# RWKV triangular systems in a hybrid decoder step: DRAM transfers replaced by VectorE 32x32 block transposes, and key norms from four products with a tile of ones

## Chip, cores and metric

The kernel runs on one core of one Trainium2 chip. The metric is the device time of one execution in microseconds (us). TensorE is called PE, VectorE DVE, ScalarE ACT, GpSimd POOL and SyncE SP, as in the profile. SP issues nearly all DMA transfers.

## The reference

One inference step of a two-layer trunk with width 1024, for one prompt of 16 + 1024 tokens and 8 sample sequences of 8 tokens: 1104 columns in all. Layer 0 is a gated DeltaNet, layer 1 is RWKV-7 time mixing. The change is in layer 1. Cut to what matters there:

```python
xs = xn[None] + xx[None] * mu[:, None, None, :]          # six mixes with the token before
rkvz = jnp.einsum('sbtd,sde->sbte', xs[:4], w_rkvz)      # r, k, v, z
...
kk = l2norm((k * k_k).reshape(B, T, H, N))               # H = 16 heads of N = 64
k = k * (1.0 + (a - 1.0) * k_a)
decay = jnp.exp(-jnp.exp(w))
b_h = kk * a_h
def step(S, inp):
    r_t, k_t, v_t, d_t, kk_t, b_t = inp
    S = (S * d_t[:, :, None, :]
         + jnp.einsum('bhvk,bhk->bhv', S, -kk_t)[..., None] * b_t[:, :, None, :]
         + v_t[..., None] * k_t[:, :, None, :])
    return S, jnp.einsum('bhvk,bhk->bhv', S, r_t)
```

The kernel does not step token by token. It takes chunks of 64 tokens. Within a chunk, the term with `-kk_t` makes a triangular system of 64 x 64 for each head. The kernel inverts those systems ahead of the recurrence.

## The kernel before

Tokens lie along the free axis, features along the partitions, and a tile holds a pair of heads: head 0 in partitions 0 to 63, head 1 in 64 to 127. The columns are cut into three segments (`SEGS`: 384, 384 and 336). One segment of one head pair is an **item**: 3 x 8 = 24 items, each with 6 chunks of 64 tokens.

The order of instructions on each engine is fixed when the program is built. A planner simulates the engines and takes ready instructions by their place in the program. Each engine then works strictly in its own order, and waits where a semaphore is not yet there. Only the recurrence has PE's order written by hand.

Layer 1 (`layer1`, L1801) runs in three parts:

1. `keys_decay_rate` (L1165) projects the keys and makes decay and rate; it stores them to DRAM as `kd`, `csd` and `ad`.
2. The loop at L1811 runs 24 projections of 128 features each (`project`, L1152): r, then v, then z. Every weight tile of 128 x 512 is loaded (`wraw`), split by ACT into `whi` and by POOL into `wlo`, and multiplied in three products for precision. Before each kind, `mix` (L1017) makes the mixed inputs on ACT, DVE and POOL. Between the projections, after numbers 1, 4, 7, 10 and 13, one batch of the inverses is put into the program (`rwkv_inverse`, L1293): five items, four in the last.
3. `wave` (L1841) runs the recurrence, with the output projection filled in. For each item `rwkv_front` (L1340) loads what the earlier parts left.

`rwkv_inverse` does this for each item of a batch:

- It loads `cs`, `a` and `k` (three DMAs of 192 KB, the next item's ahead of time). ACT scales `k` by `k_k` (tile `skk`) and makes two exponentials (`sDp`, `siD`) and the squares (`sgl`).
- DVE makes `sal` = `skk` x `sDp` (L1285); POOL corrects the first columns (L1286, L1288) and multiplies `skk` by `a` (L1310); DVE multiplies that by `siD` (L1311). Both results are stored to DRAM (`ald`, `bkd`).
- PE makes the 64 x 64 products of both (12 matmuls, PSUM tile `fL`), and the sums of squares with the mask `hmask` (one matmul of 384 columns, PSUM tile `frss`).
- ACT copies the products (L1322), POOL masks the first chunk of segment 0 (L1324), and they go to the DRAM tensor `rltd`. DVE copies the norms (L1327), and they go to `rssd`.

Then, for the batch:

- `block_scale` (L489) loads the norms back in two layouts; one is transposed by PE (`fbpp`).
- `inverse_blocks` (L457) loads the two diagonal 32 x 32 blocks of each system with one system to a partition (`invA`, at most 120 partitions) and the off-diagonal block `L21`. DVE scales `invA` (L470). `inverse32` (L442) inverts all blocks at once in 31 steps of two DVE instructions each, between `invA` and `invT`.
- ACT copies the inverse with its two free axes exchanged (L472). It is stored to DRAM (`r_u`), and so is the plain one (`r_t`). Both are loaded back into `T1n` (two DMAs a batch, L480) and `sTT` (four DMAs an item, L486), whose zero quarter POOL clears (L484).
- `inverse_merge` (L506) makes the off-diagonal block of the inverse with 2 x 12 small matmuls an item (PSUM tiles `mY`, `mU`), a DVE scaling (L518) and two ACT copies. POOL scales the result by the norms (L1336), and one DMA stores it to `ttd` (L1337).

Of the kernel before, what the change touches and what calls it, by code (L numbers as in the profile page):

```python
# [35 lines left out]
class Builder:  # L36
# [76 lines left out]
    def consts(self):  # L113
# [15 lines left out]
        self.hmask = t(cp, [128, 2], "hmask")  # L129
        nc.gpsimd.memset(self.hmask, 0.0)  # L130
        for h in (0, 1):
            nc.gpsimd.memset(self.hmask[64 * h:64 * h + 64, h:h + 1], 1.0)
# [323 lines left out]

    def inverse_blocks(self, name, ltd, scale_blk, pool, TT, T1n, L21, nth):  # L457

        nc = self.nc
        nb = 4 * nth
        for p in (0, 1):
            nc.sync.dma_start(L21[64 * p:64 * p + 32], ltd[:, 64 * p:64 * p + 32, 32:64].rearrange("c s i -> s c i"))
        A = self.t(pool, [128, 1024], "invA", 2)[0:nb]
        Av = A.rearrange("p (s i) -> p s i", i=32)
        fl = ltd.rearrange("t q i -> (t q) i").rearrange("(c s) i -> c s i", s=64)
        for r in (0, 1):
            nc.sync.dma_start(Av[2 * nth * r:2 * nth * (r + 1)], fl[:, 32 * r:32 * r + 32, 32 * r:32 * r + 32])
        nc.vector.tensor_tensor(Av, Av, scale_blk.unsqueeze(1).broadcast_to([nb, 32, 32]), op=ALU.mult)  # L470
        Tv = self.inverse32(Av, nb, pool)
        nc.scalar.copy(Av, Tv.rearrange("p i j -> p j i"))  # L472
        ud = self.dram([nb, 1024], name + "_u")
        t1d = self.dram([nb // 2, 1024], name + "_t")
        nc.sync.dma_start(ud, A)
        nc.sync.dma_start(t1d, Tv[0:nb // 2].rearrange("p i j -> p (i j)"))
        uv = ud.rearrange("(r c p) (s i) -> r p s c i", r=2, p=2, s=32)
        tv = t1d.rearrange("(c p) (s i) -> p s c i", p=2, s=32)
        for p in (0, 1):
            nc.sync.dma_start(T1n[64 * p:64 * p + 32], tv[p])  # L480
        for n, tt in enumerate(TT):
            k = tt.shape[1]
            for p in (0, 1):
                nc.gpsimd.memset(tt[64 * p + 32:64 * p + 64, :, 0:32], 0.0)  # L484
                for r in (0, 1):
                    nc.sync.dma_start(tt[64 * p + 32 * r:64 * p + 32 * r + 32, :, 32 * r:32 * r + 32],  # L486
                                      uv[r, p][:, k * n:k * n + k])

    def block_scale(self, ssd, col, pool):  # L489


        nc = self.nc
        n = col.shape[1]
        row = self.t(pool, [128, 128], "invR", 1)[0:n]
        nc.sync.dma_start(row, ssd)
        ps = self.ps("f", 2, "bpp")
        self.transpose(ps[0:128, 0:n], row)
        blk = self.t(pool, [4 * n, 32], "bblk", 2)
        for r in (0, 1):
            nc.sync.dma_start(blk[2 * n * r:2 * n * r + 2 * n], ssd.rearrange("c (p r i) -> r (c p) i", p=2, r=2)[r])  # L500
        for x, y in ((col, ps[0:128, 0:n]), (blk, blk)):
            nc.vector.tensor_scalar(x, y, 1e-6, None, op0=ALU.add)
            nc.vector.reciprocal(x, x)
        return blk

    def inverse_merge(self, L21, TT, T1n, scale_col, pool, th0, n):  # L506
# [15 lines left out]
        for c in range(n):  # L522
            for p in (0, 1):
                a = 64 * p
                self.mm(uv[a:a + 32, c, :], Y[a + 32:a + 64, c, :], TT[a + 32:a + 64, c, 32:64])
        for p in (0, 1):
            a = 64 * p
            self.act(TT[a:a + 32, :, 32:64], uv[a:a + 32], AF.Identity, scale=-1.0)

# [682 lines left out]
    def rwkv_masks(self, ap, first=False):  # L1212
# [14 lines left out]
        if first:  # L1227
            self.m_strs2 = t(ap, [128, 64], "m_strs2")
            mask(self.m_strs2, True)
            return  # L1230
# [17 lines left out]
    def rwkv_open(self):  # L1248
        self.rk2 = self.t(self.cp, [128, 144], "rk2")
        self.csd, self.ad, self.rd, self.vd, self.zd, self.kd = (self.dram([8, 128, 1152], n) for n in  # L1250
                                                                 ("csd", "ad", "rd", "vd", "zd", "kd"))
        self.ttd, self.ald, self.bkd = (self.dram([24, 128, 384], n) for n in ("ttd", "ald", "bkd"))

    def rwkv_load(self, n, pool, tag, names):
        nc, t = self.nc, self.t
        s, p = divmod(n, 8)
        c0 = SEGS[s][0]
        ld = {}
        for nm in names:
            d = {"cs": self.csd, "a": self.ad, "r": self.rd, "v": self.vd, "k": self.kd}[nm]  # L1260
            ld[nm] = t(pool, [128, 384], tag + "ld" + nm, 2 if nm in "rv" or tag == "s" else 1)
            nc.sync.dma_start(ld[nm], d[p][:, c0:c0 + 384])
        return ld

    def rwkv_keys(self, p, ld, pool, tag):

        nc, t = self.nc, self.t
        kk = t(pool, [128, 384], tag + "kk", 2)
        self.act(kk, ld["k"], AF.Identity, scale=self.pcol["rwkv_k_k"][:, p:p + 1])
        return kk, *self.rwkv_decays(ld, pool, tag)  # L1270

    def rwkv_decays(self, ld, pool, tag):

        nc, t = self.nc, self.t
        Dp, iD = t(pool, [128, 385], tag + "Dp", 1), t(pool, [128, 384], tag + "iD", 1)
        nc.gpsimd.memset(Dp[:, 0:1], 1.0)
        self.act(Dp[:, 1:385], ld["cs"], AF.Exp, scale=-self.DEC)
        self.act(iD, ld["cs"], AF.Exp, scale=self.DEC)
        return Dp, iD

    def alpha(self, al, kk, Dp, s, eng):

        nc = self.nc
        c6 = lambda x: x.rearrange("p (c k) -> p c k", k=64)
        eng.tensor_tensor(al, c6(kk), c6(Dp[:, 0:384]), op=ALU.mult)  # L1285
        nc.gpsimd.tensor_copy(al[:, :, 0:1], c6(kk)[:, :, 0:1])  # L1286
        if s == 0:
            nc.gpsimd.tensor_copy(al[:, 0, :].rearrange("p (b r) -> p b r", r=8)[:, :, 0:1],  # L1288
                                  kk[:, 0:64].rearrange("p (b r) -> p b r", r=8)[:, :, 0:1])
# [3 lines left out]
    def rwkv_inverse(self, b, pool):  # L1293

        items = range(5 * b, min(5 * b + 5, 24))
        nth = 6 * len(items)
        nc, t = self.nc, self.t
        ltd, ssd = self.dram([nth, 128, 64], f"rltd{b}"), self.dram([nth, 128], f"rssd{b}")
        for q, n in enumerate(items):
            s, p = divmod(n, 8)  # L1300
            names = ("cs", "a", "k")
            ld = self.ahead or self.rwkv_load(n, pool, "s", names)
            kk, Dp, iD = self.rwkv_keys(p, ld, pool, "s")

            self.ahead = self.rwkv_load(n + 1, pool, "s", names) if n < 23 else None
            sq = t(pool, [128, 384], "sgl", 2)
            self.act(sq, kk, AF.Square)
            al = t(pool, [128, 6, 64], "sal", 1)
            self.alpha(al, kk, Dp, s, nc.vector)
            nc.gpsimd.tensor_tensor(kk, kk, ld["a"], op=ALU.mult)  # L1310
            nc.vector.tensor_tensor(kk, kk, iD, op=ALU.mult)  # L1311
            nc.sync.dma_start(self.ald[n], al.rearrange("p c k -> p (c k)"))
            nc.sync.dma_start(self.bkd[n], kk)
            gp = self.ps("f", 2, "L")
            ssp = self.ps("f", 2, "rss")
            for c in range(6):
                for h in (0, 1):
                    a = 64 * h
                    self.mm(gp[a:a + 64, 64 * c:64 * c + 64], kk[a:a + 64, 64 * c:64 * c + 64], al[a:a + 64, c, :])
            self.mm(ssp[0:2, 0:384], self.hmask, sq)  # L1320
            gl = t(pool, [128, 6, 64], "sgl", 2)
            nc.scalar.copy(gl, gp[:, 0:384].rearrange("p (c i) -> p c i", i=64))  # L1322
            if s == 0:
                nc.gpsimd.tensor_tensor(gl[:, 0, :], gl[:, 0, :], self.m_strs2, op=ALU.mult)  # L1324
            nc.sync.dma_start(ltd[6 * q:6 * q + 6].rearrange("c q i -> q c i"), gl)
            kc = t(pool, [2, 384], "rkc", 1)
            nc.vector.tensor_copy(kc, ssp[0:2, 0:384])  # L1327
            nc.sync.dma_start(ssd[6 * q:6 * q + 6].rearrange("c (h i) -> h c i", h=2), kc.rearrange("h (c i) -> h c i", c=6))
        rk2 = self.rk2[:, 30 * b:30 * b + nth]
        blk = self.block_scale(ssd, rk2, pool)  # L1330
        TT = [t(pool, [128, 6, 64], "sTT", 3) for _ in items]
        T1n, L21 = t(pool, [128, 30, 32], "T1n", 1), t(pool, [128, 30, 32], "L21", 1)
        self.inverse_blocks(f"r{b}", ltd, blk, pool, TT, T1n[:, 0:nth], L21[:, 0:nth], nth)
        for q, n in enumerate(items):
            self.inverse_merge(L21, TT[q], T1n, rk2[:, 6 * q:6 * q + 6], pool, 6 * q, 6)
            nc.gpsimd.tensor_tensor(TT[q], TT[q], rk2[:, 6 * q:6 * q + 6].unsqueeze(2).broadcast_to([128, 6, 64]), op=ALU.mult)  # L1336
            nc.sync.dma_start(self.ttd[n], TT[q].rearrange("p c k -> p (c k)"))  # L1337


    def rwkv_front(self, p, s):  # L1340
# [11 lines left out]
        ld = self.rwkv_load(P.n, fp, "f", ("cs", "k", "a", "r", "v"))  # L1352
# [7 lines left out]
        nc.sync.dma_start(AR[:, 0].rearrange("p c k -> p (c k)"), self.ald[P.n])  # L1360
# [616 lines left out]
```

## Time and profile before

| | |
|---|---|
| Time, median of 3 runs | 2362.39 us (2358.83 to 2364.0) |
| Time of the profiled execution | 2362.64 us |
| Mean granted PE clock of the span | 0.964 |
| First and last DVE step of the RWKV inverses (start) | 1545.2 and 1820.8 us |
| First load of the recurrence (`fldk`) | 1854.8 us |
| DMA, whole span | 308.89 MB in 499719 packets, 208089 of them under 512 bytes |

The span is the time from the first to the last instruction. In the page, times of engines are busy times; "share" is busy time over the span. Rows by groups of instructions read: line, engine, operation, tile written and tiles read with their shapes, count, busy us, mean ns of one, and after the second bar the idle time of the engine just before them with what ended it. Rows by stretch give the length, then the busy time of each engine in the order of the heading, the granted PE clock, the share of the DMA engines and GB/s. Rows of waits give total us, times, and the longest. `PEld` is PE's weight load. PE records come in pairs here: a float32 matmul leaves two.

### The profile page before, as it was taken

What the parts mean: (1) busy time and instruction counts of PE and PEld (TensorE: products, weight loads), DVE (VectorE), ACT (ScalarE), POOL (GpSimd) and SP (SyncE); (2) the same over time, 40 slices, a digit from 0 to 9 for tenths busy, and PEclk for the clock granted to TensorE, in tenths of its full rate; (3) what the DMA queues carried; (4) which work ended last, traced back from release to release, by engine and by line L of the source; (5) the groups of instructions that cost most, each with busy time, mean ns of one, the idle gap of its engine ahead of it and who ended that gap; (6) DMA issues with size and microseconds to landing.
All of it is one profiled execution on the core that took longest, in us unless ns stands there. A gap on an engine that the chain in (4) does not pass through costs nothing. (4 is left out here: it accounts for less than half of the span.)

```text
span 2360.9 us, 54503 instructions
## 1 busy us (share of the span) xinstructions
PE 2167.1 (92%) x19737; PEld 1961.9 (83%) x19737; DVE 1571.2 (67%) x4219; ACT 1282.6 (54%) x3599; POOL 949.4 (40%) x1318
## 2 busy tenths in 40 slices
PE   6989999999999999999999999999888888899886
PEld 5888989889898989898989998887777866778775
DVE  6878677685858686774345833479878456667754
ACT  5455545564656555456333746646444355677763
POOL 3445333443435353434232523446445423344433
PEclk9999999999999999999999999998999998999998
DMA  3423332323233333335152145577774654677753
GB/s 113 107 76 104 88 94 78 101 75 105 78 101 91 90 102 88 109 90 184 48 163 83 52 163 175 182 199 197 188 181 130 178 160 143 178 220 227 215 153 126
DMA packets 499719, 308.89 MB, mean 131 GB/s; under 512 B 208089, under 2 KB 484826, under 8 KB 499450
## 3 DMA queue, kind: packets, MB, share of 16 engines
q1 hardware_dynamic: 499450, 305.41, 45.6%
q8 instruction: 156, 2.56, 0.5%
q14 instruction: 113, 0.93, 0.1%
HBM read 209.97 MB, written 95.33 MB: 129 GB/s over the span
## 5 line engine op out<-in xcount | busy, mean ns | idle before, releaser
L90 POOL TENSOR_TENSOR wlo<-wraw,whi 128x512 fp32r<-128x512 f32 (+2 forms) x252 | 332.4, 1322 | 359.8 <-ACT whi L86 334.4
L76 PE MATMUL d<-xc,whi 128*128 128x384 f32 (+2 forms) x910 | 260.2, 344 | 8.1 <-ACT whi L86 3.6
L86 ACT CAST whi<-wraw 128x512 fp32r<-128x512 f32 (+2 forms) x252 | 151.7, 603 | 138.8 <-PE dq L76 50.7
L419 DVE SCALAR_TENSOR_TENSOR cvy<-raw,cw,cvy 128x408 f32<-128x408 f32 (+2 forms) x288 | 178.3, 632 | 15.7 <-ACT cvy L62 13.8
L452 DVE TENSOR_TENSOR invtmp<-invA,invT 72x31 f32<-72x31 f32 (+31 forms) x403 | 172.7, 429 | 18.7 <-POOL invT L447 8.0
L76 PEld LDWEIGHTS d<-xc,whi 128*128 128x128 f32 (+1 forms) x910 | 168.9, 193 | 15.2 <-ACT whi L86 4.7
L454 DVE TENSOR_TENSOR invT<-invT,invtmp 72x31 f32<-72x31 f32 (+31 forms) x403 | 172.3, 428 | 6.6
L76 PE MATMUL dz<-xc,whi 128*128 128x384 f32 (+1 forms) x480 | 149.4, 343 | 0.0
L76 PE MATMUL dv<-xc,whi 128*128 128x384 f32 (+1 forms) x480 | 146.8, 335 | 0.0
L76 PE MATMUL d<-xa,whi 128*128 128x384 f32 (+3 forms) x450 | 141.4, 348 | 4.1 <-DVE xa L90 2.8
L76 PE MATMUL d<-xc,wlo 128*128 128x384 f32 (+2 forms) x428 | 143.9, 345 | 0.7 <-POOL wlo L90 0.7
L868 POOL TENSOR_SCALAR Sb<-Sb,eglb 128x128 f32<-128x128 f32 x128 | 80.4, 645 | 87.6 <-DMA Sb<-in_state_gdn 36.6
L76 PE MATMUL dz<-xa,whi 128*128 128x384 f32 (+1 forms) x288 | 100.3, 348 | 0.0
L76 PE MATMUL dv<-xa,whi 128*128 128x384 f32 (+1 forms) x288 | 99.9, 347 | 0.1
L76 PEld LDWEIGHTS d<-xa,whi 128*128 128x128 f32 (+1 forms) x450 | 85.2, 194 | 12.8 <-issue 5.2
L76 PEld LDWEIGHTS dz<-xc,whi 128*128 128x128 f32 x480 | 89.5, 192 | 0.8
L76 PEld LDWEIGHTS dv<-xc,whi 128*128 128x128 f32 x480 | 88.6, 188 | 0.5 <-issue 0.4
L76 PE MATMUL d<-xa,wlo 128*128 128x384 f32 (+3 forms) x252 | 86.6, 344 | 0.0
L62 ACT ACTIVATE o<-rA,gcol 128x128 f32<-128x128 f32 x128 | 46.6, 372 | 72.6 <-DVE S L779 72.0
L76 PE MATMUL d<-xh,wlo 128*128 128x384 f32 (+1 forms) x256 | 83.9, 343 | 2.0 <-POOL wlo L90 2.0
L76 PEld LDWEIGHTS d<-xc,wlo 128*128 128x128 f32 (+1 forms) x428 | 82.1, 194 | 4.0 <-issue 1.9
L76 PE MATMUL d<-xh,whi 128*128 128x384 f32 (+1 forms) x256 | 84.5, 344 | 0.5 <-ACT whi L86 0.5
(509 smaller groups left out, 7012.3 us busy)
## 6 DMA issues: line engine op xcount, KB each, us to landing
wraw<-in_gdn_w_in SPq DMA_DIRECT2D x96, 256.0 KB
wraw<-in_rwkv_w_rkvz SPq DMA_DIRECT2D x80, 256.0 KB
Sb<-in_state_gdn SPq DMA_DIRECT2D x64, 256.0 KB
wraw<-in_rwkv_w_o SPq DMA_DIRECT2D x40, 256.0 KB
E<-drow SPq DMA_DIRECT2D x24, 384.0 KB
attn<-drow SPq DMA_DIRECT2D x24, 384.0 KB
wraw<-in_gdn_w_out SPq DMA_DIRECT2D x36, 256.0 KB
out_s_gdn<-Sb SPq DMA_DIRECT2D x32, 256.0 KB
```

The lines of the kernel that those rows point to most:

```text
L62: return self.nc.scalar.activation(out, in_, func, bias=bias, scale=scale, **kw)
L76: self.nc.tensor.matmul(out, lhsT, rhs, start=start, stop=stop)
L86: nc.scalar.copy(hi, x)
L90: e.tensor_tensor(lo, x, hi.bitcast(F32), op=ALU.subtract)
L419: nc.vector.scalar_tensor_tensor(y[:, 0:wd], raw[:, k:k + wd], cw[k], y[:, 0:wd], op0=ALU.mult, op1=ALU.add)
L452: nc.vector.tensor_tensor(tmp, A[:, j, j + 1:32].unsqueeze(2).broadcast_to([nb, n, m]), Tv[:, j, 0:m].unsqueeze(1).broadcast_to([nb, n, m] ...
L454: nc.vector.tensor_tensor(Tv[:, j + 1:32, 0:m], Tv[:, j + 1:32, 0:m], tmp, op=ALU.subtract)
L868: nc.gpsimd.tensor_scalar(Sb[:, u], Sb[:, u], self.eglb[:, hv, 4 * g + u:4 * g + u + 1], None, op0=ALU.mult)
```

## The change

The RWKV inverse no longer uses DRAM between the products and the merged inverse. The recurrence is not touched, but for its loads.

- **Products.** The matmuls of an item write the two row blocks of a head apart: for each chunk and head one of 32 rows by 64 columns, and one of 32 rows by 32 columns that puts the second diagonal block under the first. ACT copies the diagonal blocks of an item into a batch tile `GD` (one buffer) and the off-diagonal ones into `L21` (two buffers, two copies). The mask of segment 0 is applied to these tiles.
- **Blocks.** Once a batch, one DVE block transpose of 1024 elements turns `GD` into `A`. All 128 partitions now hold systems. `inverse32` is as before, on a view of `A` with strides.
- **Inverses.** Two DVE block transposes of 1024 elements each write `T1n` and the diagonal part of `TD`, a batch tile with one buffer that takes the place of the `sTT` tiles. In `TD` the halves of the lower rows are exchanged, so the store to `ttd` takes six DMAs an item.
- **Norms.** Four matmuls of 192 columns with a 64 x 32 tile of ones (`hones`) give the sums in every partition of a block; a DVE block transpose from PSUM turns them to columns, and `rk2` is kept for each batch. A second, small transpose makes the scales of `A`.
- **Loads and stores.** `cs`, `a`, `k` lie side by side in one DRAM tensor and so do `r`, `v`; each group is one DMA. The load tile has a fourth slot: `al` and `bk` are made in place there and stored by one DMA to `abd`. The recurrence's loads follow this: `cak` with one buffer, `rv` with two.
- **Place.** The batches stand after projections 0, 3, 6, 9 and 12, not 1, 4, 7, 10 and 13.

```diff
-        for p in (0, 1):
-            nc.sync.dma_start(L21[64 * p:64 * p + 32], ltd[:, 64 * p:64 * p + 32, 32:64].rearrange("c s i -> s c i"))
...
-        nc.sync.dma_start(ud, A)
-        nc.sync.dma_start(t1d, Tv[0:nb // 2].rearrange("p i j -> p (i j)"))
...
-            nc.sync.dma_start(T1n[64 * p:64 * p + 32], tv[p])
...
-                self.mm(uv[a:a + 32, c, :], Y[a + 32:a + 64, c, :], TT[a + 32:a + 64, c, 32:64])
+                self.mm(uv[a:a + 32, c, :], Y[a + 32:a + 64, c, :], TT[a + 32:a + 64, c, 0, :])
...
+            x = t(pool, [128, y + len(g), 384], tag + "ld" + g, 1 if g == "cak" and tag == "f" else 2)
+            nc.sync.dma_start(x[:, y:], d[p][:, :, c0:c0 + 384])
...
-            nc.sync.dma_start(self.ald[n], al.rearrange("p c k -> p (c k)"))
-            nc.sync.dma_start(self.bkd[n], kk)
+            nc.vector.tensor_tensor(bk, kk, bk, op=ALU.mult)
+            nc.sync.dma_start(self.abd[n], ab.rearrange("p x k -> p (x k)"))
...
-                    self.mm(gp[a:a + 64, 64 * c:64 * c + 64], kk[a:a + 64, 64 * c:64 * c + 64], al[a:a + 64, c, :])
-            self.mm(ssp[0:2, 0:384], self.hmask, sq)
+                    self.mm(gp[a:a + 32, o:o + 64], bk[a:a + 64, o:o + 32], al[a:a + 64, c, :])
+                    self.mm(gp[a + 32:a + 64, o:o + 32], bk[a:a + 64, o + 32:o + 64], al[a:a + 64, c, 32:64])
+            g3 = gp[:, 0:384].rearrange("p (c x i) -> p x i c", c=6, x=2)
+            nc.scalar.copy(GD[:, :, C], g3[:, 0])
+            for a in (0, 64):
+                nc.scalar.copy(L21[a:a + 32, C], gp[a:a + 32, 0:384].rearrange("p (c x i) -> p x c i", c=6, x=2)[:, 1])
...
+            for x in range(4):
+                a = 64 * (x // 2)
+                self.mm(sp[32 * x:32 * x + 32, 0:192], self.hones[a:a + 64], sv[a:a + 64, x % 2])
+            nt = t(pool, [128, 6, 32], "rkc", 1)
+            nc.vector.transpose(nt.rearrange("p c i -> p (c i)"), sp[:, 0:192])
+            nc.vector.tensor_scalar(rk2[:, C], nt[:, :, 0], 1e-6, None, op0=ALU.add)
...
+        nc.vector.reciprocal(rk2, rk2)
+        nc.vector.transpose(blk, rk2)
...
+        nc.vector.transpose(flat(A), flat(GD))
+        nc.vector.tensor_tensor(A, A, blk.unsqueeze(2).broadcast_to([128, 32, 32]), op=ALU.mult)
+        Tv = self.inverse32(A.rearrange("p i s -> p s i"), 128, pool)
...
+        nc.vector.transpose(T1n.rearrange("p c j -> p j c"), Tv.rearrange("p i j -> p j i"))
+        nc.vector.transpose(TD[:, :, 0, :].rearrange("p c i -> p i c"), Tv)
...
-            nc.sync.dma_start(self.ttd[n], TT[q].rearrange("p c k -> p (c k)"))
+            for a in (0, 64):
+                nc.sync.dma_start(d[a:a + 32], TT[a:a + 32])
+                for x in (0, 1):
+                    nc.sync.dma_start(d[a + 32:a + 64, :, x], TT[a + 32:a + 64, :, 1 - x])
...
-            if n in (1, 4, 7, 10, 13):
-                self.rwkv_inverse((1, 4, 7, 10, 13).index(n), ip)
+            if n in (0, 3, 6, 9, 12):
+                self.rwkv_inverse((0, 3, 6, 9, 12).index(n), ip)
```

More of the change, by code (lines that the diff above doesn't have):

```diff
@@ L1248, in rwkv_open @@
     def rwkv_open(self):
[L1249 to L1252, printed above, removed]
+        self.cakd, self.rvd, self.zd = (self.dram([8, 128, n, 1152], m) for n, m in ((3, "cakd"), (2, "rvd"), (1, "zd")))
+        self.csd, self.ad, self.kd = (self.cakd[:, :, x] for x in range(3))
+        self.rd, self.vd = (self.rvd[:, :, x] for x in range(2))
+        self.zd = self.zd[:, :, 0]
+        self.ttd, self.abd = self.dram([24, 128, 384], "ttd"), self.dram([24, 128, 768], "abd")
     def rwkv_load(self, n, pool, tag, names):
@@ L1305, in rwkv_inverse @@
             self.ahead = self.rwkv_load(n + 1, pool, "s", names) if n < 23 else None
[L1306 removed]
+            sq = t(pool, [128, 384], "ssq", 1)
             self.act(sq, kk, AF.Square)
[L1308 to L1309 removed]
+            nc.vector.tensor_tensor(ab[:, 0, 1:384], kk[:, 1:384], ab[:, 0, 1:384], op=ALU.mult)
+            nc.gpsimd.tensor_copy(al[:, :, 0:1], kk.rearrange("p (c k) -> p c k", k=64)[:, :, 0:1])
@@ L1331, in rwkv_inverse @@
[L1331 to L1337 removed]
+                    a, o = 64 * h, 64 * c
@@ new lines, in rwkv_inverse @@
+        nc.vector.reciprocal(rk2, rk2)
+        blk = t(pool, [128, 32], "bblk", 1)
+        nc.vector.transpose(blk, rk2)
+        A = t(pool, [128, 32, 32], "invA", 1)
+        flat = lambda x: x.rearrange("p a b -> p (a b)")
+        nc.vector.transpose(flat(A), flat(GD))
+        nc.vector.tensor_tensor(A, A, blk.unsqueeze(2).broadcast_to([128, 32, 32]), op=ALU.mult)
+        Tv = self.inverse32(A.rearrange("p i s -> p s i"), 128, pool)
+        T1n = t(pool, [128, 32, 32], "T1n", 1)
+        if b == 0:
+            for a in (32, 96):
+                nc.gpsimd.memset(TD[a:a + 32, :, 1, :], 0.0)
```

132 lines of the change are left out of this document (50 added, 82 removed).

## The prediction

> **What bounds the kernel now.** I read the first part of the page, then busy time by stretch, then the groups that mark where the RWKV projections begin and end.
>
> ```profile
> span 2360.9 us, 54503 instructions
> PE 2167.1 (92%) x19737; PEld 1961.9 (83%) x19737; DVE 1571.2 (67%) x4219; ACT 1282.6 (54%) x3599; POOL 949.4 (40%) x1318
> ```
> ```profile
> L1312 SPq DMA_DIRECT2D ald<-sal x24: 319/332/493, 1479.1 to 1750.9; - x24
> L1163 SPq DMA_DIRECT2D zd<-ev x16: 319/338/573, 1783.3 to 1863.7; - x16
> ```
> ```profile
> core 0: us, PE busy (x) PEld busy (x) DVE busy (x) ACT busy (x) POOL busy (x), PEclk, DMA share, GB/s
> 1480.00:1864.00 384.00, 352.24 (x3289) 313.11 (x3289) 280.68 (x576) 188.43 (x407) 182.81 (x255) 0.93 0.67 179
> 1500.00:1545.00 45.00, 45.00 (x347) 40.35 (x345) 9.09 (x19) 18.63 (x40) 16.15 (x31) 1.00 0.79 212
> 1545.00:1821.00 276.00, 247.10 (x2448) 215.50 (x2445) 240.35 (x507) 138.71 (x299) 139.50 (x179) 0.93 0.68 178
> 1821.00:1864.00 43.00, 40.14 (x382) 38.12 (x381) 14.70 (x26) 15.65 (x32) 17.99 (x36) 0.92 0.62 179
> ```
>
> The first inverse item is stored at 1479 us and the last projection at 1864 us. The change lives in those 384 us; the recurrence that follows only loads what they leave. PE is the bound there: it works 352 us, stands idle 32 us, and its granted clock is 0.93, worth another 0.07 x 384 = 27 us. VectorE is the second: busy 240 of 276 us while inverses run, but only 9 of the 45 us before and 15 of the 43 us after.
>
> What makes PE idle is read from its waits in this stage (total us, times, longest):
>
> ```profile
> PE fL L76 <- DVE skk L1311: 9.8, 5, 4.1
> PE mU L76 <- issue: 4.7, 3, 2.9
> PE mY L76 <- DMA T1n<-r_t: 4.1, 2, 3.8
> PE d L76 <- ACT whi L86: 3.6, 2, 2.8
> PE mY L76 <- issue: 2.9, 1, 2.9
> PE frss L76 <- DVE invtmp L452: 2.4, 1, 2.4
> PE fbpp L73 <- DMA invR<-rssd: 0.9, 1, 0.9
> ```
>
> Each is an instruction of an inverse (or a projection's weight) that stands in PE's order ahead of projections that could run. Two of them need the timeline to be placed:
>
> ```profile
> 1722.58 0.62 ACT L86 CAST whi<-wraw 128x512 fp32r<-128x512 f32 x1 [6.67 <-DMA wraw<-in_rwkv_w_rkvz]
> ...
> 1821.07 2.11 ACT L472 COPY invA<-invT 96x1024 f32<-96x1024 f32 x1 [5.97 <-DVE invT L454]
> ...
> 1827.31 0.28 PE L76 MATMUL mY<-T1n,L 32*32 32x32 f32 x2 [2.86 <-issue]
> ```
>
> The 2.8 us wait for `whi` is a weight that landed late, while SyncE's queue worked through the inverse's small transfers. The "issue" wait of `mY` ends 4 us after ScalarE's copy of the last inverse: that is the trip of the inverse through DRAM. Now the stretches around the big gaps, first the three of DRAM, then the five of VectorE:
>
> ```profile
> 1589.00:1602.00 13.00, 9.25 (x69) 7.73 (x70) 7.63 (x17) 9.40 (x21) 6.14 (x7) 0.61 0.63 111
> 1720.00:1728.00 8.00, 4.70 (x17) 3.83 (x16) 6.59 (x13) 3.29 (x7) 4.17 (x5) 0.79 0.73 148
> 1824.00:1834.00 10.00, 7.14 (x44) 6.27 (x43) 1.98 (x5) 2.08 (x5) 3.76 (x3) 0.66 0.68 159
> ```
> ```profile
> 1640.00:1647.00 7.00, 4.62 (x35) 3.14 (x35) 6.79 (x10) 3.84 (x9) 4.75 (x6) 0.76 0.73 222
> 1659.00:1667.00 8.00, 5.61 (x34) 4.85 (x30) 4.46 (x11) 4.35 (x7) 3.07 (x6) 0.79 0.44 106
> 1683.00:1691.00 8.00, 5.32 (x39) 4.26 (x39) 7.77 (x13) 3.53 (x8) 5.21 (x8) 0.79 0.77 224
> 1749.00:1759.00 10.00, 5.99 (x36) 4.62 (x37) 9.74 (x20) 2.70 (x7) 6.41 (x8) 0.66 0.75 201
> 1792.00:1800.00 8.00, 4.99 (x63) 4.53 (x62) 7.74 (x14) 4.15 (x11) 5.32 (x8) 0.79 0.33 93
> ```
>
> Idle time is the length less PE's busy time; the clock takes (1 - PEclk) of the length on top. DRAM gaps: 3.75 + 3.30 + 2.86 = 9.9 us idle, and 13 x 0.39 + 8 x 0.21 + 10 x 0.34 = 10.2 us of clock: **20 us**. VectorE gaps: 14.5 us idle and 10.1 us of clock: **25 us**. The clock doubles the price of a gap of some 3 us.
>
> **The change, part by part.** Durations for it come from the groups of this stage:
>
> ```profile
> L1336 POOL TENSOR_TENSOR sTT<-sTT,rk 128x384 f32<-128x384 f32 x24 | 23.3, 969 | 22.3 <-ACT sTT L62 19.9 <-DMA ald<-sal 1.4 <-POOL sTT L484 0.3
> L76 PE MATMUL fL<-sal,skk 64*64 64x64 f32 x576 | 25.5, 235 | 9.8 <-DVE skk L1311 9.8
> L76 PE MATMUL frss<-sgl,hmask 128*2 128x384 f32 x48 | 21.4, 529 | 2.4 <-DVE invtmp L452 2.4
> L518 DVE TENSOR_TENSOR invY<-mY,rk 32x192 f32<-32x192 f32 x48 | 17.2, 358 | 15.9 <-PE mY L76 14.6
> L76 PE MATMUL mY<-T1n,L 32*32 32x32 f32 x576 | 15.7, 199 | 7.0 <-DMA T1n<-r_t 4.1 <-issue 2.9
> L1327 DVE COPY rkc<-frss 2x384 f32<-2x384 f32 x24 | 13.1, 544 | 1.0 <-PE frss L76 0.2
> L1322 ACT COPY sgl<-fL 128x384 f32<-128x384 f32 x24 | 11.4, 476 | 15.7 <-PE fL L76 6.7 <-DMA sTT<-r_u 3.8 <-issue 2.6
> L484 POOL MEMSET sTT<- 32x192 f32 x42 | 10.6, 252 | 26.4 <-DMA ttd<-sTT 25.0
> L472 ACT COPY invA<-invT 120x1024 f32<-120x1024 f32 (+1 forms) x5 | 10.5, 2091 | 11.3 <-DVE invT L454 11.3
> L470 DVE TENSOR_TENSOR invA<-invA,bblk 120x1024 f32<-120x1024 f32 (+1 forms) x5 | 6.1, 1221 | 5.6 <-DMA invA<-rltd 5.6
> ```
>
> *DRAM trips.* Products to blocks, inverses to merge operands, and norms no longer pass through DRAM, so the `T1n` and `invR` waits cannot occur. The late weight should go too, because SyncE issues far less:
>
> ```profile
> rltd<-sgl SPq DMA_DIRECT2D x24, 192.0 KB
> ttd<-sTT SPq DMA_DIRECT2D x24, 192.0 KB
> ...
> sTT<-r_u SPq DMA_DIRECT2D x96, 24.0 KB
> ```
>
> The 96 `sTT`, 24 `rltd`, as many norm stores and eleven more in each of five batches vanish (199); three loads of an item become one and two stores one (-72); the store of `ttd` becomes six (+120). Net 151 fewer. What that extra store could delay is the weight load behind it; I count it nothing because the queue is shorter. Taken: -20 us, and -2 us for `fbpp` (five transposes and the 0.9 us wait). Bounds: -17 if the late weight stays (its stretch is worth 3.3 + 1.7 us), and no more than the -22 of all that DRAM costs PE here.
>
> *Products on PE.* Each item has 24 products instead of 12: half stay 64 columns wide, half have 32. In the trace a record of `fL` costs 25.5 / 576 = 44 ns, one of `mY` (32 wide) 15.7 / 576 = 27 ns. If the new halves overlap as the two partition halves do now, nothing is added; if not, 24 x 24 x 27 ns = 16 us. There is no row between, so I take the middle, +8. At worst every record costs an `fL`: +25.
>
> The Trainium skill, "TensorE: Matmul & The Clock Gate", section "The mechanism", says that weights are loaded under running products only where the row group differs. The new products of one head's half share their rows, so by that rule the products cost the full 16 us, the sum is -6 instead of -14 and the time 2357 us. The rows of before hold no such products and cannot show it.
>
> *Norms on PE.* One product of 384 columns by all rows becomes four of 192 columns by half the rows, half the columns each. Two at a time, as `fL`'s halves run, that is the same 21.4 us: 0. All four at once: -11. One after another, 768 columns: +21.
>
> *VectorE.* Added per batch are three 32x32 block transposes of 1024 elements. Nearest row: `invA`, the same engine and 1024 elements, 1.22 us; 15 make +18 us. Above, ScalarE's copy that reads the same strides as two of them, 2.09 us: +31; below, half of 1.22: +9. Per item a 0.54 us copy becomes a 192-element transpose (as `invY`, 0.36) and a six-element add, about even. A batch's two pairs of add and reciprocal shrink a little; I count nothing. On the path: 0, since VectorE is idle 103 of 384 us, and the earlier place of each batch (one projection sooner) with `al` no longer waiting for a single buffer's store lets items fill the empty 1500 to 1545. If that cover is missing, the 18 us come out as lateness at `fL`.
>
> *ScalarE and POOL.* ScalarE copies three times per item instead of once (at most 48 x 0.476 = 23 us) and loses the 10.5 us copy; it is idle 196 us. POOL loses 10.6 us of memsets with their 25 us wait for `ttd` and gains a few small masks. Both 0.
>
> *Added wait.* The block tile is single: the first item of a batch is copied by ScalarE only after VectorE transposed the batch before, which follows the inverse before that. Behind it on ScalarE stand `whi` casts, which PE's projections need. Today the norm copies tie items to VectorE in the same way, so 0, up to a 4 us gap with its clock, 7 us.
>
> *Recurrence.* Five loads per item become two, prefetched: 0. No row shows a load of 576 KB; at worst one lands as late as the weight above, +7, and with fewer issues ahead of them the loads may win as much, -7.
>
> Sum: -20 - 2 + 8 + 0 = **-14 us**. The profiled execution took 2362.64 us (span 2360.9 and 1.7 around it), the median is 2362.39, so both give **2348 us**.
>
> **The rivals.**
> 1. *VectorE takes the place of DRAM.* For: it is 87% busy (240 of 276) where the inverses run and causes the larger gaps already. Against: 36 idle us before. Price: its 18 us, none of it hidden: -14 + 18, **2367 us**, no change that can be told.
> 2. *PE pays for the split.* For: PE is the bound, so each us counts, and a half's new products read the same rows. Against: the overlap that `fL` shows (576 records of 235 ns in 25.5 us). Products +25 and norms +21 instead of +8 is 38 more: **2387 us**, slower. It decides once PE's added work passes the 22 us of DRAM.
> 3. *VectorE's gaps go too*, since items run ahead and nothing stands between VectorE and the merges: -25 more, **2323 us**. Against: `fL` still waits for a VectorE, POOL, VectorE chain.
> 4. That the change does not do what it says can be left out: the removed transfers are plain in the diff.
>
> **How the numbers follow.** Forecast (2336 to 2357) 0.42; rival 1 (2358 to 2367) 0.15; rival 2 and milder forms of it 0.28; rival 3 0.15. Faster by over 0.2% is 0.42 + 0.15 = 0.57, within 0.2% (4.7 us, about what a measurement can tell here) 0.15, slower 0.28. The range runs from 2325, which leaves out about half of rival 3 (0.08), to 2380, which leaves out a third of rival 2 (0.09). The forecast's own range is 2336 to 2357.
>
> **What would show it.** Right: no PE wait for `T1n`, the stage some 14 us shorter, granted clock about 0.95, projections again the bound. The products' group near 33 us and the norms' near 21 confirm the PE terms; 50 and 43 mean rival 2. Transposes near 1.2 us confirm VectorE's; if PE's waits for VectorE grow from 14 to 25 us or more, it is rival 1. Wrong altogether would be a move outside this stage: the DeltaNet layer or the recurrence longer by over 5 us.

## The result and the profile after

The changed kernel takes **2360.11 us** (median of 20 runs, 2347.33 to 2369.11), the kernel before 2361.51 us (20 runs, 2352.62 to 2374.59): ratio 0.9995, 95% interval 0.998 to 1.001. Nothing that can be measured has changed, where a gain of 14 us was forecast. The profiled execution took 2359.64 us.

The page's head and the intervals of the stage (from the first stored item to the last stored projection: 1484 to 1866.5 us, before 1479 to 1864):

```profile
span 2357.9 us, 55429 instructions
...
PE 2159.2 (92%) x20452; PEld 1959.9 (83%) x20452; DVE 1592.9 (68%) x4248; ACT 1284.4 (54%) x3642; POOL 932.5 (40%) x1268
```
```profile
core 0: us, PE busy (x) PEld busy (x) DVE busy (x) ACT busy (x) POOL busy (x), PEclk, DMA share, GB/s
1484.00:1866.50 382.50, 340.54 (x3991) 307.03 (x3989) 306.02 (x605) 189.00 (x449) 165.24 (x208) 0.94 0.49 145
1500.00:1530.00 30.00, 28.72 (x363) 26.23 (x362) 13.14 (x22) 16.54 (x41) 13.86 (x29) 1.00 0.66 200
1530.00:1815.00 285.00, 247.15 (x3074) 220.67 (x3072) 260.51 (x530) 143.72 (x342) 120.32 (x131) 0.93 0.46 135
1815.00:1866.00 51.00, 48.67 (x438) 47.13 (x437) 19.88 (x34) 16.18 (x36) 21.18 (x39) 0.97 0.64 186
```

PE has less to do: busy 340.5 us where it was 352. But it stands idle 382.5 - 340.5 = 42 us where it was 32. So what PE saved came back as idle time, and the stage is as long as it was. VectorE is busy 25 us longer (306 for 281) and 91% of the interval with inverses (260.5 of 285). The DMA share fell from 0.67 to 0.49. What PE waits for in the stage (total us, times, longest):

```profile
PE mY L76 <- DVE T1n L1306: 9.2, 5, 2.1
PE fL L76 <- DVE sldcak L1264: 6.1, 4, 1.9
PE d L76 <- POOL wlo L90: 3.4, 4, 1.2
PE mU L76 <- DVE invY L465: 3.2, 3, 1.1
PE d L76 <- ACT whi L86: 2.7, 3, 1.6
PE d L76 <- DVE xc L90: 2.6, 1, 2.6
PE fL L76 <- DMA ttd<-sTD: 2.4, 1, 2.4
PE fL L76 <- DVE invtmp L448: 2.4, 1, 2.4
...
PE d L76 <- DVE xl L90: 2.0, 2, 1.2
```

The DRAM waits (`T1n<-r_t`, `invR`) are gone, as forecast. In their place each of the five batches now waits for VectorE's transpose (`mY` for `T1n`, 9.2 us); VectorE's waits sum to 9.2 + 6.1 + 3.2 + 2.6 + 2.4 + 2.0 = 25.5 us in the rows shown. The new groups:

```profile
L76 PE MATMUL fL<-sldcak 64*32 64x64 f32 (+1 forms) x1152 | 25.9, 216 | 14.9 <-DVE sldcak L1264 6.1 <-DMA ttd<-sTD 2.4 <-DVE invtmp L448 2.4
...
L76 PE MATMUL frss<-ssq,hones 64*32 64x192 f32 x192 | 17.7, 355 | 0.0
...
L1306 DVE STREAM_TRANSPOSE T1n<-invT 128x1024 f32<-128x1024 f32 x5 | 10.2, 2042 | 0.1
...
L1307 DVE STREAM_TRANSPOSE sTD<-invT 128x1024 f32<-128x1024 f32 x5 | 9.7, 1946 | 0.0
...
L1299 DVE STREAM_TRANSPOSE invA<-sGD 128x1024 f32<-128x1024 f32 x5 | 6.2, 1243 | 0.4 <-ACT sGD L1274 0.3
```

Products cost PE 25.9 us (25.5 before), norms 17.7 (21.4), transposes VectorE 26.1.

### The profile page after: what moved, and what is told of

It is laid out like the page before. It is cut to its first block, busy times and chain, and to the rows that moved or that the text cites. A ratio compares the mean times of both kernels' runs of the same rounds, so it can differ in the third digit from the quotient of the medians.

```text
span 2357.9 us, 55429 instructions
## 1 busy us (share of the span) xinstructions
PE 2159.2 (92%) x20452; PEld 1959.9 (83%) x20452; DVE 1592.9 (68%) x4248; ACT 1284.4 (54%) x3642; POOL 932.5 (40%) x1268
## 5 line engine op out<-in xcount | busy, mean ns | idle before, releaser
L415 DVE SCALAR_TENSOR_TENSOR cvy<-raw,cw,cvy 128x408 f32<-128x408 f32 (+2 forms) x288 | 178.3, 632 | 15.8 <-ACT cvy L62 13.9
L76 PE MATMUL d<-xl,whi 128*128 128x384 f32 (+1 forms) x256 | 84.0, 345 | 2.1 <-DVE xl L90 2.0
```

The source lines that it names most:

```text
L76: self.nc.tensor.matmul(out, lhsT, rhs, start=start, stop=stop)
L415: nc.vector.scalar_tensor_tensor(y[:, 0:wd], raw[:, k:k + wd], cw[k], y[:, 0:wd], op0=ALU.mult, op1=ALU.add)
```

## The experiments

All times are medians; each ratio is to the kernel before on the same chip, with its 95% interval. Each edit also lets the planner set the order of every engine anew, and no run here separates that from the edit itself. First theories: **A**, VectorE's new work took back what DRAM gave; **B**, PE's fixed order costs the same whatever VectorE has to do.

**The DRAM trip alone** (kernel before):

```diff
-        uv = ud.rearrange("(r c p) (s i) -> r p s c i", r=2, p=2, s=32)
+        uv = self.eyed[0:nb].rearrange("(r c p) (s i) -> r p s c i", r=2, p=2, s=32)
...
+        return Av          # read by the merges in place of T1n
```

> The kernel before with the trip of the inverse through DRAM cut off from the merges: the merges read the copy that ScalarE makes of the inverse, and the diagonal blocks come from a stored identity, by as many DMAs of the same size; VectorE's work stays as it was. The inverses that reach the recurrence are so not the reference's. Theory A (VectorE's added work took back what DRAM gave): the two T1n gaps go, 3.75 + 2.86 us idle and 5.1 + 3.4 us of clock, about 15 us: 2347 us (2342 to 2352). Theory B (PE's fixed order: the merge waits for VectorE where it waited for DRAM, whatever VectorE's load): at most 5 us faster, 2357 to 2363, with new waits of mY for the copy or for invT.

Measured: 2359.94 us, 0.9992 (0.9978 to 1.0007). Its waits show what took the trip's place:

```profile
PE fL L76 <- DVE skk L1318: 12.6, 5, 4.6
PE mY L76 <- ACT invA L472: 6.5, 3, 3.9
PE fbpp L73 <- DMA invR<-rssd: 2.4, 2, 1.4
```

The `T1n` wait is gone, and the merges wait 6.5 us for the copy behind VectorE's last step instead; `fL` waits 12.6 us for VectorE (9.8 before). So the two gaps that I had priced at 15 us were worth 2, at most 5. That speaks against A, in which the trip should pay as long as VectorE's work is unchanged.

**VectorE's transposes: twice, or on ScalarE** (changed kernel):

```diff
+        nc.vector.transpose(T1n...)      # both strided transposes once more
...
-        nc.vector.transpose(...)         # the other kernel: both as
+        nc.scalar.copy(...)
```

> The changed kernel with the two strided transposes of each batch issued twice, 10 x 2.0 = 20 us more for VectorE, 4 us later merges in each batch. Theory A: VectorE is the bound while inverses run, so 20 us more in its work come out at the end: about 2380 us (2373 to 2385). Theory B: the planner knows the longer transposes and puts the merges later, so PE does other work meanwhile: 2356 to 2366.

> The changed kernel with the two strided transposes of each batch made into ScalarE copies of the same views (2.1 us each by the copy of before), which leaves out the 32x32 transposition itself, so the inverses are not the reference's. VectorE has 20 us less to do, the way from the last inverse step to the merge stays as long. Theory A: 20 us faster, about 2340 us (2336 to 2348). Theory B: the merges wait as before, only for ScalarE: 2354 to 2364.

Measured: twice 2371.63 us, 1.004 (1.0024 to 1.0056); on ScalarE 2362.88, 1.0002 (0.9982 to 1.0021). 20 us more cost 11, and 20 us less gave nothing. On ScalarE PE's waits for `whi` were 5.2 us and for `invY` 8.4 (2.7 and 3.2 in the changed kernel), so ScalarE's queue may hide a gain. The same relief without another busy engine:

```diff
-        nc.vector.transpose(T1n.rearrange("p c j -> p j c"), Tv.rearrange("p i j -> p j i"))
-        nc.vector.transpose(TD[:, :, 0, :].rearrange("p c i -> p i c"), Tv)
+        nc.gpsimd.tensor_copy(TD[:, :, 0, :], self.eyeb.unsqueeze(1).broadcast_to([128, 32, 32]))
```

The merges then read `invT` itself, which gets a second buffer.

> The changed kernel without the two strided transposes: the merges read the inverse as it stands, and the diagonal blocks are an identity that POOL writes (the inverses are not the reference's). VectorE has 20 us less to do, 4 us less stand between the last step and each merge, and no other engine's queue that feeds PE gets the work (POOL gets five copies). Theory V (VectorE's new work took back what DRAM gave): 2340 to 2350 us. Rival C (it is another part, ScalarE's copies or SyncE's six stores an item): 2355 to 2363.

Measured: 2354.76 us, 0.9978 (0.9961 to 0.9995), 4 us below the changed kernel. Theory A falls in this form: 20 us of transposes are worth about 4. PE was not free of VectorE in this kernel either, since its merges now wait for the last steps of the inverse:

```profile
PE mY L76 <- DVE invT L450: 20.2, 16, 3.4
```

**Other places in PE's order** (changed kernel): the merges later in the program, VectorE out of their middle, both, and the batches' old place.

```diff
+            if n in (6, 10, 13, 17, 21):   # merges of batch b, then inverse of batch b + 1
...
-            nc.vector.tensor_tensor(Y[a:a + 32], yv[a:a + 32], scale..., op=ALU.mult)
+            nc.scalar.copy(Y[a:a + 32], yv[a:a + 32])
...
-            if n in (0, 3, 6, 9, 12):
+            if n in (1, 4, 7, 10, 13):
```

> The changed kernel with the merges of each batch put later in the program, after projections 6, 10, 13, 17 and 21, about one projection after VectorE has its inverse; the steps of the next batch's inverse follow them in the program. VectorE's work is the same. Theory A: VectorE's amount of work decides, nothing changes or the later inverses cost some: 2357 to 2370 us. Theory B: the waits of mY (9.2 us) and mU (3.2 us) go, with about 10 us of clock: about 2338 us (2333 to 2345); the waits of fL stay.

> The changed kernel with VectorE out of the merge's middle: ScalarE copies Y from PSUM, and the norms that VectorE multiplied there are put on the diagonal blocks by POOL before the merge, which is the same product. VectorE has 17 us less to do (48 x 0.36). Theory V: the wait of mU for invY (3.2 us idle) and a part of the waits of fL go, 5 to 15 us faster: about 2350 us. Theory O: mU waits for ScalarE instead, 2356 to 2364.

> The deferred merges of before (after projections 6, 10, 13, 17 and 21) with VectorE out of their middle (Y copied by ScalarE, norms on the diagonal blocks). In the deferred kernel mU waited 15.2 us for invY. Theory V: those waits and mY's go and VectorE has 17 us less: 2340 to 2350 us. If ScalarE's queue takes VectorE's place: 2358 to 2373.

> The changed kernel with the batches after projections 1, 4, 7, 10 and 13, as before the change. If the earlier place is what covers VectorE's 28 us of new work, the later place costs a part of them: 2368 us or more (up to 2385). If the place is neutral, as theory V with VectorE's queue as the bound from the second batch on would have it: 2356 to 2364.

Measured: deferred 2373.01 us, 1.0047 (1.0031 to 1.0062); `Y` by ScalarE 2363.17, 1.0013 (0.9999 to 1.0027); both 2372.0, 1.0056 (1.0036 to 1.0077); old place 2365.82, 1.0027 (1.0013 to 1.0042). In the deferred kernel `mY` waits for nothing any more, but:

```profile
PE mU L76 <- DVE invY L465: 15.2, 7, 4.5
PE fL L76 <- DVE sldcak L1264: 7.9, 6, 2.1
PE d L76 <- ACT whi L86: 6.5, 5, 2.6
```

Theory B expected 22 us of gain, and the kernel lost 12: wherever the merges stand, the next instruction that needs VectorE finds it late. Not all of the loss lies there. The stage is 4 us longer (386.5 for 382.5), and behind it the first product of the recurrence waits 7.5 us for its loads, which SyncE issues only from 1873.9 us on, after the stores of the last, deferred batch (1871.8; in the changed kernel 1845.7 and 1844.4). The earlier place is worth some 7 us to the changed kernel by the ratios (1.0027 against 0.9995). In the kernel before it is worth nothing:

> The kernel before with its batches after projections 0, 3, 6, 9 and 12. The changed kernel lost about 7 us when it was put back to the old place. If the place is worth that by itself: about 2353 us (2350 to 2356). If only the changed kernel gains by it, since in the kernel before the items wait for DRAM and single buffers: 2357 to 2365.

Measured: 2360.29 us, 1.0007 (0.9995 to 1.002).

**Both causes together.** Theory **V**: DRAM's trip and VectorE's lateness cover each other, so that one taken away shows the other. One edit halves the inverse steps in each kernel, and one adds the cut trip to it. I had reckoned with 72 us less work for VectorE; its busy time in the stage fell by 60 us (281 to 221 before, 306 to 245 in the changed kernel).

```diff
-        for j in range(31):
+        for j in range(0, 31, 2 if nb > 72 else 1):     # RWKV's inverses only
```

> The kernel before with only every second step of the RWKV inverse (16 of 31; half the elimination is left out, the inverses are not the reference's): about 72 us less VectorE work in the stage, and nothing else changed. Theory V (VectorE paces the stage: whatever another cause gives up, PE waits for VectorE instead): the VectorE gaps of 25 us go, the DRAM gaps of 20 us now stand uncovered: about 2337 us (2330 to 2345). Theory O (PE's fixed order costs the same whatever VectorE has to do): 2357 to 2365.

> The same relief in the changed kernel (16 of 31 steps). Theory V: now the DRAM trips that the change removed can pay, so it is 15 to 20 us faster than the relieved kernel before, about 2318 us (2312 to 2328). Theory D (the DRAM trips never cost anything): within 5 us of the relieved kernel before. Theory O: 2355 to 2363.

> The kernel before with the inverse's DRAM trip cut off from the merges and, in the same kernel, 16 of 31 inverse steps (inverses not the reference's). One alone gave -2 us and the other +7. Theory V, two causes that cover each other, with the trip of the inverse as the DRAM part: both together pay, 2338 to 2350 us. If the DRAM part is SyncE's queue and the norms' trip instead: 2355 to 2366.

| kernel | all 31 steps | 16 steps |
|---|---|---|
| before | 1 | 1.0032 (1.0016 to 1.0048), 2366.13 us |
| before, trip cut | 0.9992 (0.9978 to 1.0007) | 0.9939 (0.992 to 0.9958), 2346.07 us |
| changed | 0.9995 (0.998 to 1.001) | 0.9929 (0.9914 to 0.9945), 2342.01 us |

This carries the explanation. Neither alone makes the kernel before faster; both together give 14 us. With VectorE relieved, the change is worth 2366 - 2342 = 24 us, about what I had forecast for DRAM (20 + 2). In the relieved kernel before, DRAM's waits are larger than they were (`T1n` and `invR` 11.5 us, where it was 5.0), and so are those for `whi` (8.8, where it was 3.6):

```profile
PE fL L76 <- DVE skk L1311: 9.9, 4, 4.8
PE d L76 <- ACT whi L86: 8.8, 5, 2.7
PE mY L76 <- DMA T1n<-r_t: 6.0, 3, 2.1
PE fbpp L73 <- DMA invR<-rssd: 5.5, 3, 4.2
```

Before the five `whi` casts ScalarE waited for a loaded weight only once, for 0.2 us; they stood behind its other work. I had expected this kernel 25 us faster, and it was 7 slower. The waits show that other causes took VectorE's place; why it even lost is not settled.

**Why VectorE is late.** Its busy time grew by 25 us. To see how much of that is work, I took for each VectorE instruction of the stage its duration above the shortest of the same line and shape, and added these up; this excess is called *stretch* from here on. The last batch of the kernel before fills 96 partitions and the others 120, so its steps are compared with the same steps of the others. (The 21 us beside `wlo` that the expectation for the kernel before names below leave that comparison out.) The stretch is 71 us before and 77 us in the changed kernel. Nearly all of it lies beside an operation of POOL, 30 and 33 us beside `wlo`. So VectorE's own work is 281 - 71 = 210 us before and 306 - 77 = 229 after: **19 of the 25 us are work, 6 are stretch.** The work is the new transposes (26.1 us, and 10 us of small ones for the norms) less the 13.1 us of norm copies and some 4 us elsewhere. The inverse steps, which carry most of the stretch, take 148 us in both kernels; in the kernel before:

```profile
L452 DVE TENSOR_TENSOR invtmp<-invA,invT 120x31 f32<-120x31 f32 (+25 forms) x155 | 75.2, 485 | 11.5 <-POOL invT L447 8.0
...
L454 DVE TENSOR_TENSOR invT<-invT,invtmp 120x31 f32<-120x31 f32 (+25 forms) x155 | 73.1, 472 | 3.8
```

So the change did not bring the stretch. It is a quarter of VectorE's busy time in both kernels. One such place in the changed kernel, VectorE's timeline and then POOL's (start, us):

```profile
1553.99 0.41 DVE L448 TENSOR_TENSOR invtmp<-invA,invT 128x252 f32<-128x252 f32 x1
1554.44 1.55 DVE L450 TENSOR_TENSOR invT<-invT,invtmp 128x252 f32<-128x252 f32 x1
1556.03 1.39 DVE L448 TENSOR_TENSOR invtmp<-invA,invT 128x247 f32<-128x247 f32 x1
1557.45 0.42 DVE L450 TENSOR_TENSOR invT<-invT,invtmp 128x247 f32<-128x247 f32 x1
```
```profile
1554.42 2.72 POOL L90 TENSOR_TENSOR wlo<-wraw,whi 128x512 fp32r<-128x512 f32 x2
```

Two subtractions of POOL run from 1554.42 to 1557.14. The two VectorE steps beside them take 1.55 and 1.39 us; their neighbours of the same size take 0.41 and 0.42, and the second of them ends 0.3 us after POOL does. A transpose, which reads one tile, does not mind:

```profile
1699.41 1.27 POOL L90 TENSOR_TENSOR wlo<-wraw,whi 128x512 fp32r<-128x512 f32 x1 [5.73 <-ACT whi L86]
1699.50 1.94 DVE L1307 STREAM_TRANSPOSE sTD<-invT 128x1024 f32<-128x1024 f32 x1
```

1.94 us is its usual time (mean 1946 ns). The Trainium skill, "SBUF — State Buffer", section "Who interferes with whom", says the same: an instruction of VectorE with two inputs in SBUF contends with a GpSimd instruction that reads SBUF, not with one that only writes, and with at most one such input, outside VectorE's 2-port modes, it does not contend. The trace agrees (1.55 and 1.39 against 0.4; 1.94 against 1.95).

Theory **P**: this stretch makes VectorE late. The test moves `wlo` from POOL to VectorE in this stage:

```diff
-        w = self.load_w(self.i["rwkv_w_rkvz"][0, m][:, 128 * k:128 * k + 128])
+        w = self.load_w(self.i["rwkv_w_rkvz"][0, m][:, 128 * k:128 * k + 128], eng_lo="pool" if m == 1 else "dve")
...                                   # two further doses:
-            nc.gpsimd.tensor_tensor(kk, kk, ld["a"], op=ALU.mult)
+            nc.vector.tensor_tensor(kk, kk, ld["a"], op=ALU.mult)
...
-            nc.gpsimd.tensor_tensor(v, v, rk2[:, 6 * q:6 * q + 6]...)
+            nc.vector.tensor_tensor(v, v, rk2[:, 6 * q:6 * q + 6]...)
...
-        self.split(x, xh[:, a:b], xl[:, a:b], eng_lo="pool" if k % 2 else "dve")
+        self.split(x, xh[:, a:b], xl[:, a:b], eng_lo="pool" if k % 2 and not m in (2, 3) else "dve")
```

> The changed kernel with the low halves of the projections' weights (wlo, 47 of them in the stage) made by VectorE instead of POOL. VectorE gets 47 more subtractions of 128 x 512, about 0.7 us each by the 0.55 us of 128 x 384: +31 us of its own work. But 33 us of its busy time in the stage is what instructions beside a POOL wlo last longer than the shortest of their shape. Theory P (VectorE is late because POOL's operations hold up its instructions, which the fixed order does not reckon with): about as much work, but on time: 2340 to 2352. Rival (VectorE's amount of work alone decides): 2357 to 2366, later if the weights queue behind inverse steps.

> The changed kernel with wlo and the product of the scaled keys with a (24 operations of 1.06 us on POOL) on VectorE: another +13 us of work against 11 us of stretch. Theory P: like h_wlo or up to 5 us better, since items no longer go from POOL to VectorE, 2338 to 2350. Rival (amount of work): 2362 to 2375.

> The kernel of the second dose (wlo and the product with a on VectorE), and besides the scaling of the merged inverse by the norms (24 of 0.9 us on POOL) and the low halves of the mixed inputs of v and z (some 20 of 1.2 us): all of POOL's two-input operations of the stage but a few are VectorE's. About 25 us more work for VectorE against the 22 us of stretch that is left beside them. Theory P: 2335 to 2345. If VectorE's amount now decides: 2346 to 2360.

> The same edit in the kernel before. VectorE's stretch beside wlo is 21 us there. Theory V with P (two causes that cover each other, DRAM's trip still in place): no gain, 2358 to 2368. If the stretch of VectorE is a cost by itself: 2345 to 2355.

Measured: `wlo` on VectorE **2343.74 us, 0.9942 (0.9921 to 0.9964)**; with the product too 2342.22, 0.9933 (0.9914 to 0.9952); nearly all of POOL's operations 2356.66, 0.9976 (0.9955 to 0.9997); the kernel before with `wlo` on VectorE 2350.97, 0.9964 (0.9947 to 0.9981). The first two are faster than both kernels. The interval and the groups of the first, to the end of its stage at 1844 us:

```profile
core 0: us, PE busy (x) PEld busy (x) DVE busy (x) ACT busy (x) POOL busy (x), PEclk, DMA share, GB/s
1484.00:1844.00 360.00, 327.41 (x3953) 298.57 (x3943) 295.19 (x643) 185.95 (x441) 109.57 (x159) 0.97 0.51 151
```
```profile
L450 DVE TENSOR_TENSOR invT<-invT,invtmp 128x31 f32<-128x31 f32 (+15 forms) x155 | 66.0, 426 | 3.0
...
L448 DVE TENSOR_TENSOR invtmp<-invA,invT 128x31 f32<-128x31 f32 (+15 forms) x155 | 60.3, 389 | 3.3 <-POOL invT L443 0.2
...
L90 DVE TENSOR_TENSOR wlo<-wraw,whi 128x512 fp32r<-128x512 f32 x45 | 30.8, 684 | 7.7 <-ACT whi L86 7.7
```

In the changed kernel the steps are:

```profile
L448 DVE TENSOR_TENSOR invtmp<-invA,invT 128x31 f32<-128x31 f32 (+15 forms) x155 | 76.3, 492 | 3.3
...
L450 DVE TENSOR_TENSOR invT<-invT,invtmp 128x31 f32<-128x31 f32 (+15 forms) x155 | 71.9, 464 | 3.7
```

VectorE has 45 subtractions more (30.8 us), and its busy time is lower, 295 us for 306; the same 310 steps take 126 us for 148. Its own work grew to 247 us and its stretch fell to 48, so here the amount of work alone cannot be what decides.

The third dose shows the other side. From 1484 to 1866 us its VectorE is busy 301 us with 22 us of stretch, so its own work is 279 us (229 in the changed kernel), and most of the gain is gone. Most of that loss, 10 us of the 14 against the second dose, is one wait at the first product of the recurrence:

```profile
PE fG L76 <- DVE BK L1348: 10.2, 1, 10.2
```
```profile
L1110 SPq DMA_DIRECT2D zd<-ev x16: 325/338/1188, 1770.1 to 1838.8; - x16
L1221 SPq DMA_DIRECT2D fldcak<-cakd x24: 524/551/1854, 1858.4 to 2230.0; - x24
```

The last projection is stored at 1838.8 us, 5 us earlier than in the first dose. But the last inverse step ends at 1833.4 us, where it was 1797.8. The stores of that batch stand in SyncE's queue ahead of the recurrence's first load (`fldcak`), which goes out at 1858.4 us, where it was 1830.1; VectorE itself is idle then and waits for the load. So VectorE's amount of work counts as well as the stretch, but in this run through a late last batch that holds up the recurrence, and not through the projections.

The kernel before contradicts theory V as I had put it: it should not have gained, and gained 8 us. With VectorE on time, DRAM's waits are the larger part of what is left there, 5.4 + 5.0 + 3.5 = 13.9 us:

```profile
PE fbpp L73 <- DMA invR<-rssd: 5.4, 2, 3.0
PE fL L76 <- DVE skk L1311: 5.1, 2, 3.9
PE mU L76 <- DMA sTT<-r_u: 5.0, 2, 4.3
PE mY L76 <- DMA T1n<-r_t: 3.5, 4, 1.6
```

So the cover is not complete: relief by fewer steps gave nothing there, relief by less stretch gave 8 us. With `wlo` on VectorE in both kernels the change is worth 5 to 7 us (by the ratios, and 2350.97 - 2343.74), with half the steps it was 24; why the two differ is open. The gain of the moved `wlo` could also have come from POOL's shorter queue (124 us busy for 184). The next kernel keeps that queue long with operations that only write:

```diff
+                for _ in range(3):
+                    nc.gpsimd.memset(lo[:, 0:m, 0:n].bitcast(F32), 0.0)
```

> The changed kernel with wlo made by VectorE, and POOL kept as full as it was: before each of these subtractions POOL clears the same wlo tile three times (some 1.4 us by the 0.95 us that it takes for 1024 elements), an operation that writes and reads nothing from SBUF. Theory P as stretch (VectorE's two-input instructions wait for POOL operations that read): the gain stays, 2338 to 2350 us, and few VectorE instructions last longer beside these clears. Rival (it was POOL's own queue, where the items' products and scalings stood behind wlo): the gain goes, 2355 to 2366.

> The changed kernel with wlo on VectorE and 16 of 31 inverse steps (inverses not the reference's): 72 us less VectorE work once most of the stretch is gone. If VectorE still holds PE after the first dose: 2320 to 2332. If it doesn't, and what is left of the stage is PE's own work and its fixed order: 2336 to 2346.

Measured: with the clears 2347.51 us, 0.9951 (0.9927 to 0.9975). The gain stays, though POOL is as busy as in the changed kernel (174 us of 360; 165 of 382.5), and 5 us of stretch lie beside the clears, where 33 us lay beside the subtractions:

```profile
1484.00:1844.00 360.00, 323.00 (x3952) 293.79 (x3952) 293.95 (x645) 187.99 (x447) 174.07 (x291) 0.97 0.47 140
```
```profile
L206 POOL MEMSET wlo<- 128x512 f32 x135 | 69.9, 525 | 33.8 <-PE d L76 30.1
```

It is the stretch, not the queue. With 16 of 31 steps besides `wlo` on VectorE: 2333.18 us, 0.9872 (0.984 to 0.9904), 11 us less than with `wlo` alone by the medians and 16 by the ratios. The median lies just above the range that I had set for this case (2320 to 2332), but the intervals of the two kernels (0.984 to 0.9904 and 0.9921 to 0.9964) do not touch: VectorE still holds PE after the first dose.

## Why the prediction was wrong

- **The step that failed** is the pair "*DRAM trips* ... Taken: -20 us" and "*VectorE* ... On the path: 0, since VectorE is idle 103 of 384 us". I added the DRAM gaps up as if what ended them were the only thing that PE waited for. Cutting the inverse's trip alone, priced at 15 of those 20 us, gave 2; with VectorE relieved by 60 us, the change as a whole gave 24. The idle 103 us were no cover, since two thirds of them (103 - 36) lay where no inverse ran.
- **VectorE's sum was right, its place on the path was not.** I counted 18 us of new work and none of it on the path. The three large transposes take 26.1 us, the strided ones 2.04 and 1.95 us instead of 1.22, other parts shrank, and VectorE's own work grew by 19 us. On the path they are not nothing: 20 us more cost 11, and 20 us less gave 4. By these two doses the 19 us are worth 4 to 11 us, an estimate. What I did not see is the stretch, 71 us before the change already. I read the mean of the inverse steps and never their spread: in the changed kernel the ten `invtmp` steps of 252 elements take 0.41 to 1.24 us.
- **Rival 1** ("VectorE takes the place of DRAM") named the mechanism: PE's waits for VectorE grew from 14 to 25.5 us, the mark that I had set. Its price, the new work in full, is too high by the doses above, and its 2367 us is 7 too high.
- **PE's terms** were mis-sized on the safe side: products +0.4 instead of +8, norms -3.7 instead of 0. With them the sum would have been -20 - 2 + 0.4 - 3.7 = -25 us, and -1 was measured. The 13 us that the inverse's trip did not give and the 4 to 11 us of VectorE's work make 17 to 24 of these 24 us; this is an estimate from separate runs, which need not add up. The rule that I had quoted from the Trainium skill ("TensorE: Matmul & The Clock Gate", "The mechanism") would have made products 16 us longer; the trace shows 1152 records in 25.9 us, where 576 took 25.5. The two parts of a head's half, which share their rows, ran beside one another, so here the measurement decides against it. Rival 2 is out.
- **SyncE's shorter queue** was right in direction: the long wait for `whi` (2.8 us) is not there, though three short ones are (2.7 in all). One wait of 2.4 us for the store `ttd` is new.
- **The added wait and the recurrence** at 0 are not contradicted. From the last projection's store to the end the profiles have 491 us for 497, but the kernel before in its earlier place has 485 with the same recurrence, so I read nothing from it.
- **The earlier place** did give cover, some 7 us, and only to the changed kernel.

Open is why the kernel before lost 7 us with half its inverse steps, when less stretch made it faster. Open is also how much of each run's difference comes from the planner's new orders.

## What to carry to other kernels

Gaps of a bound engine are worth their sum only if nothing else would be late at the same place: before you price a removed wait, ask what that instruction would have waited for next, and test two suspects together as well as one by one. On an engine that looks busy, compare each group's mean with its shortest instruction of the same shape; what lies between them beside another engine's operation is not work, and moving that other operation can free more than it costs.

## What the runs showed of the hardware

- A VectorE instruction with two SBUF inputs waited for a POOL subtraction of 128 x 512 to end, 1.55 us instead of 0.4; the same subtraction costs VectorE itself 0.68 us and POOL 1.34. Beside 70 us of POOL's clears of the same tile VectorE's instructions were stretched by 5 us in all, beside 63 us of its subtractions by 33.
- A 32x32 block transpose of 128 x 1024 took 1.24 us on contiguous views and 2.04 and 1.95 us on strided ones.
- Matmuls that read the same 64 rows and write 32 output rows each ran beside one another: 1152 records in 25.9 us, as long as 576 of 64 output rows (25.5).
